# A second MLP product from seven block products instead of eight, with weights fetched in pairs

## The chip, the cores and the metric

The kernel runs on one core of a Trainium2 chip. The metric is the device time of one execution in microseconds. Before the change the median of 3 runs is 866.44 us (865.52 to 868.4).

## The reference, cut to what matters

Two layers, each a mixing sublayer and a squared-ReLU MLP, over 256 tokens of width 1024, all in float32. The change is in the second product of the MLP; the mixing sublayer (a convolution branch and two attentions, gated and projected) keeps its arithmetic.

```python
for l in range(DEPTH):                      # DEPTH = 2
    u = x @ w_in[l]
    ...                                     # y_a: convolution, y_b, y_c: attention
    m = gates[:, :, 0] * y_a + gates[:, :, 1] * y_b + gates[:, :, 2] * y_c
    x = layer_norm(DEEPNORM_ALPHA * x + m @ w_o[l], ln1_g[l], ln1_b[l])
    h = jnp.square(jax.nn.relu(x @ w_ff1[l] + b_ff1[l]))        # 256 x 4096
    x = layer_norm(DEEPNORM_ALPHA * x + h @ w_ff2[l] + b_ff2[l], ln2_g[l], ln2_b[l])
```

## The kernel before, in words

Every float32 operand of a large product is split into two float32r parts, hi and lo, whose sum is the float32 value, and each product is three matmuls (`mm3`: lo·hi, hi·lo, hi·hi). ScalarE writes hi (a cast), VectorE writes lo (a subtraction).

Weights come as units of 128 x 1024 (512 KB). `Weights.get` gives each its own raw tile (ring of RAWS = 4), hi tile and lo tile (rings of NW = 8), issues the DMA on SyncE, the cast on ScalarE and the subtraction on VectorE. In the trace these are `raw`, `whi`, `wlo`. Tiles tagged `big` (16 slots of 128 x 1024) hold the stream, its transposed split X, the hidden layer's split H, norm rows and the like; `zz` are scratch tiles; `pm`, `pa` and `pt` are the 2 + 4 + 2 PSUM banks.

A layer goes: convolution input (48 matmuls of 512 columns for each of the two token tiles), v, then q and k in `tunit`s (two chunks of 128 output columns: 48 matmuls of 256 columns from two weight units), attention beside them, gates and branch projections, output projection, first norm, MLP. In the MLP the first six 128-column chunks of the hidden layer are made with tokens on partitions and transposed; then a loop over i = 3 to 15 runs `do2(i - 3)`, 24 matmuls of 512 columns (2 k tiles, 2 token tiles, 2 halves of the output, 3 each), and a `tunit` with `hsplit(i)`, which turns two chunks into squared-ReLU and its hi and lo. The last six k tiles are done first for token tile 0, then for token tile 1 (36 matmuls each), so that the norm of tile 0 (`ln_tok`) runs while TensorE works on tile 1. The norm of a tile ends in transposes that give the next layer's X.

The order of instructions on each engine is not the order of the source. `Plan` records all instructions, computes a latest start for each from its own costs, and issues them by list scheduling: on each engine the ready instruction with the earliest latest start goes first. At run time each engine works through its list strictly in that order. Nearly every instruction is recorded through a helper, so the trace gives L122 for all; groups are told apart by their tiles.

Of the kernel before, what the change touches and what calls it, by code (L numbers as in the profile page):

```python
# [24 lines left out]
RAWS = 4  # L25
WARM = 4
NW = 8
# [13 lines left out]
class Plan:  # L41
    """Records instructions with the regions that they read and write, orders them by list
    scheduling (the one whose result is needed first goes first) and issues them in that order.
    Tile adds the waits and gives out the buffers."""
# [189 lines left out]
    def order(self):  # L234
# [20 lines left out]
        def need(op):  # L255
            """when the buffers that the instruction is first to use are free, None if unknown"""
            tm = 0.0
            new = [k for k in op.tiles if k not in where]
            seen = {}
            for k in new:  # L260
                tag = self.tiles[k]["tag"]
                j = seen.get(tag, 0)
                if self.tiles[k]["turn"] != turn[tag] + j or len(free[tag]) <= j:
                    return None
                seen[tag] = j + 1
                tm = max(tm, free[tag][j])
            return tm
# [63 lines left out]
class Weights:  # L331
    """Streams the weight units in the order of use: each lands in SBUF once and is split
    into two float32r parts whose sum is the float32 value."""
# [7 lines left out]
    def get(self, **dims):  # L341
        plan, i = self.plan, self.i
        self.i += 1
        raw = plan.tile(self.pool, [P, 1024], F32, "raw", RAWS)
        hi = plan.tile(self.pool, [P, 1024], F32R, "whi", NW)
        lo = plan.tile(self.pool, [P, 1024], F32R, "wlo", NW)
        n = 512 if i < 3 else 1024
        for c in range(0, 1024, n):
            s = slice(c, c + n)
            plan.SP.dma_start(raw[:, s], self.order[i][:, s])  # L350
            plan.Activation.copy(hi[:, s], raw[:, s])
            plan.DVE.tensor_sub(lo[:, s], raw[:, s], hi[:, s].bitcast(F32))
        pat = "p (" + " ".join(list(dims) + ["n"]) + ") -> p " + " ".join(list(dims) + ["n"])
        return [a.rearrange(pat, **dims) for a in (hi, lo)]
# [3 lines left out]
def kernel(ctx: ExitStack, tc: tile.TileContext, x, xT, w_in, w_p2, w_o, w_f1, w_f2,  # L358
# [22 lines left out]
    def split(hi, lo, src, scale=1.0):  # L381
        """hi + lo = scale * src"""
# [8 lines left out]
    def mm3(o, a, b, start, stop):  # L391
        """o += a.T @ b with a, b = (hi, lo)"""
# [62 lines left out]
    def x_at(X, kt, cols=slice(0, SEQ)):  # L455
        """(hi, lo) of k tile kt"""
# [3 lines left out]
    def rstd_of(var, n=1, eps=EPS, scale=1.0):  # L460
        """(scale * var + eps) ** -0.5"""
# [9 lines left out]
    def ln_tok(t, banks, resid, alpha, gb, dst, transposed):  # L471
        """dst = LN(alpha * resid + banks) * g + b, and its transposed split."""
        y = slot(F32, "y")
        st = R.tile(small, [P, 2, 6], F32, "st", 2)
        for h in range(2):
            s = slice(h * 512, (h + 1) * 512)
            R.DVE.scalar_tensor_tensor(y[:, s], in0=resid[:, s], scalar=alpha, in1=banks[h],
                                           op0=ALU.mult, op1=ALU.add)
# [25 lines left out]
    for l in range(L):  # L504
# [23 lines left out]
        def tunit(ticks=True):  # L528
            ps = bank()
            for c in range(2):  # L530
                w = W.get(k=KT)
                for kt in range(KT):
                    mm3(ps[:, c * 256:(c + 1) * 256], at(w, ALLP, kt), x_at(X, kt), kt == 0,
# [13 lines left out]
        # conv: gated input, then taps as background work  # L547
# [14 lines left out]
        wc = [W.get(k=2) for _ in range(8)]  # L562
# [26 lines left out]
        wv = [W.get(k=2) for _ in range(8)]  # L589
        V = [[None] * NT for _ in range(2)]  # L590
        for t in range(NT):
            for b in range(2):
# [5 lines left out]
                V[b][t] = R.tile(work, [P, 512], F32, "v", 4)  # L598
                R.Activation.copy(V[b][t], ps)

        # q, k with rotary
# [18 lines left out]
        def attn_scores(b, pair):  # L620
            """masked softmax numerators of two heads (maps), and 1 / row sums"""
# [20 lines left out]
        def transp(src):  # L642
            """[queries, keys] blocks (q1k0, q1k1, q0k0) -> (k0: q0 q1 | k1: q1), split"""
# [6 lines left out]
        # differential attention, head h  # L650
# [56 lines left out]
        # MoBA with one block: heads 2j, 2j + 1  # L707
# [39 lines left out]
        for b in range(2):  # L747
            for u in range(2):
                for w in 'qk':
                    ps = tunit()  # L750
                    d = R.tile(work, [P, 512], F32, "qk", 7)
# [48 lines left out]
        macc = [None, None]  # L800
        M = None
        for bi, gofs in ((0, 8), (1, 16), (2, 0)):
# [17 lines left out]
            for u in range(4):  # L820
                w = W.get(c=2, k=4)
                ps = bank()
                for c in range(2):
                    for kt in range(4):
                        mm3(ps[:, c * 256:(c + 1) * 256], at(w, ALLP, c, kt), at(br, ALLP, kt),
# [18 lines left out]
        gb1 = load_row(l, 0), load_row(l, 1)  # L844
        wo = [W.get(k=1) for _ in range(8)]
        X = x_new()
        for t in range(NT):
# [6 lines left out]
            ln_tok(t, ps, xtok[t], ALPHA, gb1, xtok[t], X)  # L854

# [1 line left out]
        H = {}  # L857

        def hsplit(i, ps):
            """chunks 2i, 2i + 1 of the hidden layer"""  # L860
            r = R.tile(work, [P, 1024], F32, "zz", 3)[:, :512]
            for c in range(2):
                n = 2 * i + c
                R.Activation.activation(r[:, c * 256:(c + 1) * 256], ps[:, c * 256:(c + 1) * 256],
# [157 lines left out]
```

## Time and profile before

| what | us |
|---|---|
| median of 3 runs | 866.44 |
| span of the profiled execution, first to last instruction | 867.0 |
| its time outside this span | not listed by the profile |
| TensorE (PE) busy | 852.5 |
| VectorE (DVE) busy | 624.7 |
| ScalarE (ACT) busy | 512.9 |
| GpSimd (POOL) busy | 20.6 |

The mean granted TensorE clock is 0.998 of full speed. The profiled span is 0.56 us above the median of the runs. TensorE's busy time comes from records whose ends overlap (a 512-column matmul is listed with about 0.39 us, but the next one starts 0.23 us later), so what a matmul costs is read from start to start: a stretch of the chain divided by its count. The same holds for VectorE, where a record lasts a little longer than the distance to the next start. DMA moved 157.06 MB, 181 GB/s on average.

### The profile page before, as it was taken

The page shows a single profiled execution, that of the slowest core. Times are in us where ns is not written, and L with a number is a line of the kernel's source. Part 1 is how long each engine was busy: PE and PEld are TensorE (multiplying, and loading weights), DVE is VectorE, ACT ScalarE, POOL GpSimd, SP SyncE. Part 2 cuts the span into 40 slices and gives each one's busy share as a digit, 9 for nine tenths or more (in the row PEclk, how much of TensorE's full clock was granted, in tenths as well). Part 3 has the DMA queues.
Part 4 walks back from the last instruction along what each step waited for, and adds up shares of the span by engine and source line. Part 5 has one row for each costly group of instructions (what it writes and reads, how often), then busy time and mean ns, then how long its engine had stood idle before and what let it go on. Part 6 is the DMA issues. An engine that isn't in the chain of part 4 may idle for free.

```text
span 867.0 us, 14603 instructions
## 1 busy us (share of the span) xinstructions
PE 852.5 (98%) x5704; PEld 781.1 (90%) x5704; DVE 624.7 (72%) x1011; ACT 512.9 (59%) x854; POOL 20.6 (2%) x26
## 2 busy tenths in 40 slices
PE   8999999999999999999999999999999999999996
PEld 7899989999989999999887999999998899999995
DVE  5789999985686645544588899998766874554445
ACT  5578898447347555555354788964472675555540
POOL 0000010000000000000000001000000000000000
PEclk9999999999999999999999999999999999999999
DMA  8874425554637755655365843345554686655621
GB/s 325 286 237 160 152 98 169 159 184 151 215 114 249 283 182 193 188 181 190 98 198 171 263 147 124 121 157 183 172 171 145 203 299 203 193 189 180 191 73 50
DMA packets 44422, 157.06 MB, mean 181 GB/s; under 512 B 4929, under 2 KB 5441, under 8 KB 44353
## 3 DMA queue, kind: packets, MB, share of 16 engines
q1 hardware_dynamic: 44352, 156.13, 55.4%
q8 instruction: 45, 0.74, 0.3%
q14 instruction: 25, 0.20, 0.1%
HBM read 155.06 MB, written 1.05 MB: 180 GB/s over the span
## 4 chain that ended last, share of the span: by engine, by line
PE 88%; DVE 6%; DMA 2%; ACT 2%; issue 1%; POOL 1%; DVEq 0%; ACTq 0%
PE pm L122 56%; PE pa L122 31%; DVE wlo L122 2%; DVE big L122 2%; DMA raw<-in_w_f_dram 1%; ACT zz L122 1%; DVE zz L122 1%; POOL col L122 1%; DMA raw<-in_w_in_dram 1%; DVE pt L122 1%; PE pt L122 1%; DMA big<-in_xT_dram 0%; ACT whi L122 0%; DVE qk L122 0%; DVE col L122 0%
## 5 line engine op out<-in xcount | busy, mean ns | idle before, releaser
L122 DVE TENSOR_TENSOR wlo<-raw,whi 128x1024 fp32r<-128x1024 f32 (+1 forms) x283 | 341.7, 1211 | 155.8 <-ACT whi L122 154.1
L122 PE MATMUL pm<-big,whi 128*128 128x256 f32 x2496 | 452.6, 283 | 0.0
L122 ACT CAST whi<-raw 128x1024 fp32r<-128x1024 f32 (+1 forms) x283 | 293.8, 1044 | 241.9 <-PE pm L122 169.9
L122 PEld LDWEIGHTS pm<-big,whi 128*128 128x128 f32 x2496 | 388.9, 192 | 1.3
L122 PE MATMUL pm<-big,wlo 128*128 128x256 f32 x1248 | 357.5, 286 | 0.0
L122 PEld LDWEIGHTS pm<-big,wlo 128*128 128x128 f32 x1248 | 239.0, 192 | 3.1
L122 PE MATMUL pa<-whi,big 128*128 128x512 f32 x704 | 225.1, 393 | 1.1 <-DVE big L122 1.1
L122 PEld LDWEIGHTS pa<-whi,big 128*128 128x128 f32 x704 | 133.1, 189 | 28.6 <-ACT whi L122 1.7
L122 PE MATMUL pa<-wlo,big 128*128 128x512 f32 x352 | 138.1, 392 | 0.0
L122 DVE SCALAR_TENSOR_TENSOR big<-hpad,half,big 128x256 f32<-128x256 f32 x240 | 103.5, 477 | 0.1
L122 PE MATMUL pm<-whi,big 128*128 128x512 f32 (+1 forms) x320 | 92.5, 370 | 0.0
L122 PEld LDWEIGHTS pa<-wlo,big 128*128 128x128 f32 x352 | 66.7, 190 | 12.8
L122 PEld LDWEIGHTS pm<-whi,big 128*128 128x128 f32 x320 | 58.3, 188 | 10.3 <-ACT zz L122 0.4
L122 PE MATMUL pm<-wlo,big 128*128 128x512 f32 (+1 forms) x160 | 59.3, 371 | 0.0
L122 ACT COPY zz<-pm 32x512 f32<-32x512 f32 (+1 forms) x72 | 40.8, 566 | 14.4 <-DVE zz L122 9.8
L122 DVE TENSOR_TENSOR big<-zz,big 128x512 fp32r<-128x512 f32 x32 | 22.1, 691 | 28.3 <-ACT big L122 28.3
L122 ACT ACTIVATE pt<-pt,col 128x256 f32<-128x256 f32 (+1 forms) x96 | 41.4, 461 | 0.8 <-DVE col L122 0.3
L122 POOL TENSOR_TENSOR col<-col,mhalf 128x1 f32<-128x1 f32 (+1 forms) x20 | 20.0, 1001 | 788.6 <-DVE col L122 788.6
L122 PEld LDWEIGHTS pm<-wlo,big 128*128 128x128 f32 x160 | 30.2, 189 | 4.8
L122 ACT CAST big<-pt 128x512 fp32r<-128x512 f32 x12 | 6.9, 591 | 35.8 <-PE pt L122 35.5
L122 DVE SCALAR_TENSOR_TENSOR big<-big,pa 128x512 f32<-128x512 f32 x16 | 11.0, 685 | 19.7 <-PE pa L122 19.5
L122 ACT ACTIVATE zz<-pm,cols 128x256 f32<-128x256 f32 x52 | 21.6, 465 | 4.7 <-PE pm L122 4.7
(79 smaller groups left out, 453.6 us busy)
## 6 DMA issues: line engine op xcount, KB each, us to landing
raw<-in_w_f_dram SPq DMA_DIRECT2D x128, 512.0 KB, 4.1
raw<-in_w_in_dram SPq DMA_DIRECT2D x109, 512.0 KB, 3.8
raw<-in_w_p_dram SPq DMA_DIRECT2D x24, 512.0 KB, 3.5
raw<-in_w_o_dram SPq DMA_DIRECT2D x16, 512.0 KB, 3.6
big<-in_rows_dram SPq DMA_DIRECT2D x10, 512.0 KB, 6.1
raw<-in_w_in_dram SPq DMA_DIRECT2D x6, 256.0 KB, 5.2
big<-in_xT_dram SPq DMA_DIRECT2D x4, 256.0 KB, 5.3
big<-in_x_dram SPq DMA_DIRECT2D x2, 512.0 KB, 8.1
```

The lines of the kernel that those rows point to most:

```text
L122: op.fn = lambda: fn(*args, **kw)
```

## The change: what it does

The product h @ w_ff2 is cut in two along tokens, along k within each pair of k tiles, and along output columns, and the eight block products are replaced by seven (a Strassen form with shared sums). For one pair of k tiles that is 21 matmuls of 512 columns in place of 24, and 16 pairs make a layer. For it VectorE forms four sums of weight blocks (`t`, 128 x 2048) and four differences of blocks of the hidden layer, and these are split into hi and lo like everything else: per pair of k tiles 1536 columns of plain blocks and 2048 columns of sums, where before there were two units of 1024. `hsplit` splits 896 columns where it split 512.

Weights are fetched two units into one raw tile of 128 x 2048 (RAWS = 3) and split from it, in halves of 1024 in the mixing sublayer and in one piece of 2048 in the MLP. Raw tiles apart, all weight tiles, the sums, v and the q and k tiles (until now in tiles of their own) share one ring `ws` of 11 tiles of 128 x 2048. In the list of VectorE, `ws_a<-raw_b,ws_c` is a subtraction that writes lo.

Seven accumulators take seven PSUM banks through the loop. The last DEFER = 3 pairs leave out products 7 and 4, which are recorded behind the norm of token tile 0. The norm's input is no longer one VectorE operation for each half: `fill0` and `fill1` combine the seven accumulators with the stream.

```diff
-RAWS = 4
+RAWS = 3
-NW = 8
+NW = 11
+DEFER = 3
@@ Weights
+    def split(self, raw, c0=0, c1=2048, step=2048):
+        hi, lo = self.tile(), self.tile()
+        for c in range(c0, c1, step):
+            s = slice(c, min(c + step, c1))
+            self.plan.Activation.copy(hi[:, s], raw[:, s])
+            self.plan.DVE.tensor_sub(lo[:, s], raw[:, s], hi[:, s].bitcast(F32))
+        return hi, lo
...
+    def products(self):
+        plan = self.plan
+        raw = self.load()
+        b = raw.rearrange("p (b n) -> p b n", b=4)
+        bh, bl = self.split(raw, 512)
+        t = self.tile(F32)
+        t4 = t.rearrange("p (b n) -> p b n", b=4)
+        plan.DVE.tensor_add(t4[:, 0:3:2], b[:, 1:4:2], b[:, 0:1].broadcast_to([P, 2, 512]))
+        plan.DVE.tensor_add(t4[:, 1], t4[:, 0], b[:, 3])
+        plan.DVE.tensor_add(t4[:, 3], t4[:, 1], b[:, 2])
+        th, tl = self.split(t)
...
@@ hsplit
-            t = slot(name="h").rearrange("p (s n) -> p s n", s=2)
-            H[i] = (t[:, 0], t[:, 1])
-            split(*H[i], r)
+            R.Activation.activation(f[:, 512:1024], r, AF.Square)
+            R.DVE.tensor_sub(b[:, 0:2], b[:, 5:7], b[:, 7:8].broadcast_to([P, 2, P]))
+            R.DVE.tensor_add(b[:, 2], b[:, 6], b[:, 0])
+            R.DVE.tensor_sub(b[:, 3], b[:, 2], b[:, 4])
+            hi, lo = slot(name="h"), slot(name="h")
+            split(hi[:, 0:896], lo[:, 0:896], f[:, 0:896])
@@ the loop of the MLP
-        for i in range(3, 16):
-            do2(i - 3)
-            ps = tunit()
-            hsplit(i, ps)
-        last = [W.get(k=1) for _ in range(6)]
-        for h in range(2):
-            for j in range(6):
-                ff2(26 + j, last[j], 0, h)
+        FACTORS = {1: ("a11", "b11"), 2: ("a12", "b21"), 3: ("s4", "b22"), 4: ("a22", "t4"),
+                   5: ("s1", "t1"), 6: ("s2", "t2"), 7: ("s3", "t3")}
...
+        for i in range(3, 19):
+            w = W.products()
+            for q in (1, 2, 3, 5, 6):
+                ff2(q, i - 3, w)
+            if i - 3 >= 16 - DEFER:
+                last[i - 3] = w
+            else:
+                for q in (7, 4):
+                    ff2(q, i - 3, w)
+            if i < 16:
+                hsplit(i, tunit(step=2048))
...
+        def fill0(h, y):
+            if h == 0:
+                R.Activation.copy(q1, Q[1])
+                R.DVE.tensor_add(y, r[0][0], Q[2])
+                R.DVE.tensor_add(y, y, q1)
+            else:
+                R.DVE.tensor_sub(u, Q[6], q1)
+                R.DVE.tensor_add(y, r[0][1], u)
+                R.DVE.tensor_sub(y, y, Q[5])
+                R.DVE.tensor_sub(y, y, Q[3])
...
+        ln_tok(0, fill0, gb2, xtok[0], X)
+        for q in (7, 4):
+            for i in last:
+                ff2(q, i, last[i])
+        ln_tok(1, fill1, gb2, xtok[1], X)
```

What that does to VectorE's list in the loop is seen in one round. Before, a round of the loop of layer 0 reads (`wlo`: lo of a weight unit, `big<-zz`: lo of the hidden layer):

```order
L122 TENSOR_TENSOR big_670<-zz_669,big_670 128x512
L122 TENSOR_TENSOR wlo_703<-raw_701,whi_702 128x1024
L122 TENSOR_TENSOR wlo_706<-raw_704,whi_705 128x1024
L122 TENSOR_TENSOR wlo_710<-raw_708,whi_709 128x1024
L122 TENSOR_TENSOR wlo_713<-raw_711,whi_712 128x1024
```

With the change, from one subtraction for a `tunit`'s weights to the next (`zz`: hidden-layer differences, `ws_602`: the sums, `ws_603` and `ws_604`: their hi and lo):

```order
L123 TENSOR_TENSOR zz_582<-zz_582 128x256
L123 TENSOR_TENSOR ws_601<-raw_599,ws_600 128x1536
L123 TENSOR_TENSOR ws_602<-raw_599 128x2x512
L123 TENSOR_TENSOR zz_582<-zz_582 128x128
L123 TENSOR_TENSOR ws_602<-ws_602,raw_599 128x512
L123 TENSOR_TENSOR zz_582<-zz_582 128x128
L123 TENSOR_TENSOR ws_602<-ws_602,raw_599 128x512
L123 TENSOR_TENSOR big_584<-zz_582,big_583 128x896
L123 TENSOR_TENSOR ws_604<-ws_602,ws_603 128x2048
L123 TENSOR_TENSOR ws_608<-raw_606,ws_607 128x2048
```

Four subtractions of 1024 columns and one of 512 have become ten instructions, and the subtraction `ws_604` needs a cast (`ws_603`, on ScalarE) of all four sums, the last of which is two rows above it.

At the end of the loop of layer 0, VectorE's list before reads (`pa_592`, `pa_593`: the accumulators of token tile 0; `big_811`, `big_812`: lo of the next layer's X):

```order
L122 TENSOR_TENSOR big_790<-zz_789,big_790 128x512
L122 SCALAR_TENSOR_TENSOR big_813<-big_84,pa_592 128x512
L122 BN_STATS st_814<-big_813 128x6
L122 SCALAR_TENSOR_TENSOR big_813<-big_84,pa_593 128x512
L122 BN_STATS st_814<-big_813 128x6
L122 BN_AGGR col_742_815<-st_814 128x2
L122 TENSOR_SCALAR col_743_816<-col_742_815 128x1
L122 SCALAR_TENSOR_TENSOR big_813<-big_813,col_742_815,big_590 128x512 x2
L122 SCALAR_TENSOR_TENSOR big_84<-big_813,col_744_817,big_591 128x512 x2
L122 TENSOR_TENSOR big_811<-pt_818,big_809 128x4x128
```

With the change, from the last subtraction of sums on (`pa_468` to `pa_471`: products 3, 5, 6 and 7; `ws_702` to `ws_708`: the next layer's first weights; the list goes on with three more weight subtractions, the norm's last four operations and `big_675`, `big_676`, lo of X):

```order
L123 TENSOR_TENSOR ws_672<-ws_670,ws_671 128x2048
L123 TENSOR_TENSOR ws_702<-raw_700,ws_701 128x1024
L123 TENSOR_TENSOR big_85<-big_85,pa_469 128x512
L123 TENSOR_TENSOR zz_677<-pa_470,zz_677 128x512
L123 TENSOR_TENSOR ws_702<-raw_700,ws_701 128x1024
L123 TENSOR_TENSOR big_678<-big_84,zz_677 128x512
L123 TENSOR_TENSOR zz_677<-zz_677,pa_471 128x512
L123 TENSOR_TENSOR big_678<-big_678,pa_469 128x512
L123 TENSOR_TENSOR ws_705<-raw_703,ws_704 128x1024
L123 TENSOR_TENSOR big_678<-big_678,pa_468 128x512
L123 TENSOR_TENSOR ws_705<-raw_703,ws_704 128x1024
L123 BN_STATS st_679<-big_678 128x6
```

The norm of token tile 0 used to take one operation on a finished accumulator for each half; now its second half is put together from products 5, 6 and 3 behind the last subtraction of sums, with subtractions for the next layer between the steps.

## Rows read from the trace of the kernel before

**Rows 1.** The page, part 1: span, and busy time, share and instructions of engines.
```profile
span 867.0 us, 14603 instructions
...
PE 852.5 (98%) x5704; PEld 781.1 (90%) x5704; DVE 624.7 (72%) x1011; ACT 512.9 (59%) x854; POOL 20.6 (2%) x26
```

**Rows 2.** Busy time by stretch: attention (112:158) and the loop of layer 0 (275:416.7).
```profile
core 0: us, PE busy (x) PEld busy (x) DVE busy (x) ACT busy (x) POOL busy (x), PEclk, DMA share, GB/s
112.00:158.00 46.00, 45.98 (x353) 42.55 (x352) 45.04 (x110) 38.24 (x101) 2.15 (x2) 1.00 0.46 139
275.00:416.70 141.70, 141.70 (x903) 129.28 (x902) 75.25 (x68) 78.59 (x103) 0.00 (x0) 1.00 0.63 202
```

**Rows 3.** The chain that ended last: start us, us, what, with the matmul count.
```profile
274.94 5.47 PE pa L122 x24
...
287.54 5.75 PE pm L122 x48
...
416.71 12.72 PE pa L122 x56
430.55 8.87 PE pa L122 x39
...
700.87 5.47 PE pa L122 x24
```

**Rows 4.** Groups of instructions by shape: busy us, mean ns, idle before.
```profile
L122 DVE TENSOR_TENSOR wlo<-raw,whi 128x1024 fp32r<-128x1024 f32 x277 | 337.6, 1222 | 155.4 <-ACT whi L122 153.8
L122 ACT CAST whi<-raw 128x1024 fp32r<-128x1024 f32 x277 | 290.1, 1053 | 241.2 <-PE pm L122 169.9 <-PE pa L122 38.5 <-DMA raw<-in_w_in_dram 13.0
...
L122 DVE TENSOR_TENSOR big<-zz,big 128x512 fp32r<-128x512 f32 x32 | 22.1, 691 | 28.3 <-ACT big L122 28.3
...
L122 ACT CAST big<-zz 128x512 fp32r<-128x512 f32 x32 | 20.1, 629 | 0.8
```

**Rows 5.** VectorE in order of time, first norm of layer 0: start, duration, idle.
```profile
228.87 0.68 DVE L122 SCALAR_TENSOR_TENSOR big<-big,pm 128x512 f32<-128x512 f32 x1
229.47 1.22 DVE L122 TENSOR_TENSOR wlo<-raw,whi 128x1024 fp32r<-128x1024 f32 x1
...
246.11 0.68 DVE L122 SCALAR_TENSOR_TENSOR big<-big,pa 128x512 f32<-128x512 f32 x1
...
247.43 3.48 DVE L122 TENSOR_TENSOR wlo<-raw,whi 128x1024 fp32r<-128x1024 f32 x3
251.03 0.69 DVE L122 SCALAR_TENSOR_TENSOR big<-big,pa 128x512 f32<-128x512 f32 x1
...
253.80 2.73 DVE L122 SCALAR_TENSOR_TENSOR big<-big,col,big 128x512 f32<-128x512 f32 x4
...
258.72 1.28 DVE L122 TENSOR_TENSOR big<-pt,big 128x512 fp32r<-128x512 f32 x2
```

**Rows 6.** All engines in order of time, inside the loop: a cast and its subtraction.
```profile
301.67 1.05 ACT L122 CAST whi<-raw 128x1024 fp32r<-128x1024 f32 x1 [1.83 <-PE pm L122]
...
302.75 1.23 DVE L122 TENSOR_TENSOR wlo<-raw,whi 128x1024 fp32r<-128x1024 f32 x1 [1.65 <-ACT whi L122]
```

**Rows 7.** VectorE in order of time, second norm of layer 0.
```profile
424.94 0.69 DVE L122 SCALAR_TENSOR_TENSOR big<-big,pa 128x512 f32<-128x512 f32 x1 [1.08 <-PE pa L122]
...
426.70 2.73 DVE L122 SCALAR_TENSOR_TENSOR big<-big,col,big 128x512 f32<-128x512 f32 x4
...
432.62 0.68 DVE L122 TENSOR_TENSOR big<-pt,big 128x512 fp32r<-128x512 f32 x1
```

**Rows 8.** The chain that ended last, its end, layer 1.
```profile
854.91 4.09 PE pa L122 x18
...
859.03 0.70 DVE big L122
...
862.12 0.74 DVE big L122
862.86 0.66 DVEq L1018
```

More of the change, by code (lines that the diff above doesn't have):

```diff
@@ L339, in __init__, with tile @@
         self.i = 0
[L341 to L352, printed above, removed]
-        pat = "p (" + " ".join(list(dims) + ["n"]) + ") -> p " + " ".join(list(dims) + ["n"])
-        return [a.rearrange(pat, **dims) for a in (hi, lo)]
+    def tile(self, dtype=F32R, tag="ws", bufs=NW):
+        return self.plan.tile(self.pool, [P, 2048], dtype, tag, bufs)
@@ new lines, in load @@
+    def load(self, n=1024):
+        raw = self.tile(F32, "raw", RAWS)
+        for u in range(2):
+            for c in range(0, 1024, n):
+                self.plan.SP.dma_start(raw[:, u * 1024 + c:u * 1024 + c + n],
+                                       self.order[self.i][:, c:c + n])
+            self.i += 1
+        return raw
+    def split(self, raw, c0=0, c1=2048, step=2048):
[5 more added lines that the diff above has]
+        return hi, lo
@@ new lines, in get2, with take @@
+    def get2(self, step=1024, **dims):
+        first = self.i < 4
+        raw = self.load(512 if first else 1024)
+        pair = self.split(raw, step=512 if first else step)
+        pat = "p (" + " ".join(list(dims) + ["n"]) + ") -> p " + " ".join(list(dims) + ["n"])
+        return [[a[:, u * 1024:(u + 1) * 1024].rearrange(pat, **dims) for a in pair]
+                for u in range(2)]
+    def take(self, n, step=1024, **dims):
+        return [w for _ in range(n // 2) for w in self.get2(step, **dims)]
@@ L560, in tap @@
                                                op0=ALU.mult, op1=ALU.add)
-        wc = [W.get(k=2) for _ in range(8)]
+        wc = W.take(8, k=2)
         pp = [[bank("pa"), bank("pm")] for _ in range(NT)]
@@ L586 @@
                 R.bias = 0.0
-        wv = [W.get(k=2) for _ in range(8)]
+        wv = W.take(8, k=2)
+        vt = W.tile(F32)
         V = [[None] * NT for _ in range(2)]
@@ L597 @@
                         kt == 0, kt == KT - 1)
-                V[b][t] = R.tile(work, [P, 512], F32, "v", 4)
+                V[b][t] = vt[:, (2 * b + t) * 512:(2 * b + t + 1) * 512]
                 R.Activation.copy(V[b][t], ps)
@@ L747 @@
         for b in range(2):
+            qk = W.tile(F32)
             for u in range(2):
-                for w in 'qk':
+                for i, w in enumerate('qk'):
                     ps = tunit()
-                    d = R.tile(work, [P, 512], F32, "qk", 7)
+                    d = qk[:, (2 * u + i) * 512:(2 * u + i + 1) * 512]
                     rope(ps, d)
@@ L844 @@
         gb1 = load_row(l, 0), load_row(l, 1)
-        wo = [W.get(k=1) for _ in range(8)]
+        wo = W.take(8, k=1)
         X = x_new()
@@ L909, in tick, with ff2 @@
+        Q = {}
+        for q in (1, 2, 3, 5, 6, 7, 4):
+            Q[q] = bank("pt" if q < 3 else "pm" if q == 4 else "pa")
+        def ff2(q, i, w):
+            a, b = FACTORS[q]
+            mm3(Q[q], H[i][a], w[b], i == 0, i == 15)
         def tick():
             pass
-        for i in range(3, 16):
-            do2(i - 3)
-            ps = tunit()
-            hsplit(i, ps)
-        last = [W.get(k=1) for _ in range(6)]
-        for h in range(2):
-            for j in range(6):
-                ff2(26 + j, last[j], 0, h)
@@ L920 @@
[L920 to L925 removed]
+        last = {}
+        for i in range(3, 19):
[9 more added lines that the diff above has]
+                hsplit(i, tunit(step=2048))
@@ new lines @@
+        X = x_new() if l < L - 1 else None
+        qq = R.tile(work, [P, 1024], F32, "zz", 3)
+        q1, u = qq[:, :512], qq[:, 512:]
+        r = [[xtok[t][:, h * 512:(h + 1) * 512] for h in range(2)] for t in range(NT)]
+        def fill0(h, y):
[8 more added lines that the diff above has]
+                R.DVE.tensor_sub(y, y, Q[3])
@@ L927, with fill1 @@
+        def fill1(h, y):
+            if h == 0:
+                R.DVE.tensor_sub(r[1][1], r[1][1], Q[5])
+                R.DVE.tensor_sub(u, u, Q[7])
+                R.DVE.tensor_sub(y, r[1][0], u)
+                R.DVE.tensor_add(y, y, Q[4])
+            else:
+                R.DVE.tensor_add(y, r[1][1], u)
+        ln_tok(0, fill0, gb2, xtok[0], X)
[3 more added lines that the diff above has]
+        ln_tok(1, fill1, gb2, xtok[1], X)
     for t in range(NT):
```

62 lines of the change are left out of this document (32 added, 30 removed).

## The prediction, made before the run

> **What bounds the kernel now.** I read the busy shares first, then the stretches, the chain, the groups by shape and last the single instructions. TensorE is busy for 852.5 of 867.0 us [rows 1], and in the loop of layer 0 for all 141.7 us at a granted clock of 1.00, while VectorE is busy for 75.25 [rows 2]. The chain alternates between 24 matmuls of 512 columns in 5.47 us, 0.228 us each, and 48 of 256 columns in 5.75 us, 0.120 us each [rows 3]. A round is therefore 11.22 us, all TensorE, and VectorE has about half of it free. The large idle time in front of VectorE's subtractions is put down to ScalarE's casts (153.8 us) [rows 4]; in the loop it costs nothing now. The question is whether it still costs nothing once VectorE's half-empty rounds are filled.
>
> **Matmuls removed.** 3 of 24 in each of 16 pairs and 2 layers: 96 x 0.228 = 21.9 us of TensorE's path. With nothing else in the way a round is 21 x 0.228 + 5.75 = 10.54 us. The second product of layer 0 ends now at 416.71 + 72 x 0.228 + 0.9 for eight transposes in between = 434.0; the next layer's convolution starts right there (430.55 + 8.87 - 24 x 0.228 = 433.9) [rows 3]. With 48 matmuls fewer TensorE alone would be through at 423.0.
>
> **VectorE's work added.** What an operation costs in a full queue is the distance of starts, not its duration. One of 512 columns takes 0.60 (228.87 to 229.47); of 1024 columns, three in a row take 3.48 and the last of them 1.22, so 1.13 each [rows 5]. That is 0.53 for 512 more columns, and I go along this line to the sizes that the trace does not show: 2048 columns 2.19, 1536 1.66, 896 1.00, 256 0.33, 128 0.20. For 2048 the bounds are 4 x 0.53 = 2.12 (columns alone) and 2 x 1.22 = 2.44 (two of the shown ones, full duration [rows 4]); I take 2.19, on the line of the starts. A broadcast operand is not shown either: between 1.13 and two of 0.69 for the sum of 1024 columns; I take 1.13, the nearest shape.
> A round is now: plain blocks 1.66, sums 1.13 + 0.60 + 0.60, their subtraction 2.19, the `tunit`'s weights 2.19, hidden layer 0.33 + 0.20 + 0.20 + 1.00. Together 10.1 us, against 4 x 1.13 + 0.60 = 5.1 before. This alone fits under TensorE's 10.54, with 0.44 us to spare.
>
> **The wait added.** The subtraction of the sums waits for one cast of all four sums, and that cast for the last sum. A cast of 1024 columns takes 1.05, of 512 0.63 [rows 4], so 2048 take 1.05 + 2 x 0.42 = 1.90. A subtraction starts 0.03 after its cast ends (301.67 + 1.05, then 302.75) [rows 6]; for the step from VectorE to ScalarE I take 0.05. From the start of the last sum: 0.69 + 0.05 + 1.90 + 0.03 = 2.67, of which the sum itself takes 0.60 of the queue. In the remaining 2.07 VectorE can only do what its list has between the two. In the 15 pairs behind the first that is a piece of 128 columns six times (1.87 idle), the 896-column subtraction five times (1.07 idle), and in the other four 0.93, 0.94, nothing and 1.37. Sum 19.8 us in a layer. Queued behind the waiting instruction are the next `tunit`'s weights, which TensorE waits for. A round is then 10.1 + 1.55 = 11.65 us: longer than TensorE's 10.54, and longer than the 11.22 of before. Below, the wait could cost nothing, if VectorE were so far ahead that TensorE never saw it; but VectorE is the slower one in each round, so a lead is used up, by 1.1 us a round.
>
> **The start of the loop.** In the first norm VectorE's list has 3.48 + 1.13 us of weight subtractions between 246.11 and the norm's last operations, which end at 253.80 + 2.73 = 256.5 [rows 5]. Now there are 2048 + 2048 + 1536 + 1024 + 512 columns, 7.8 us, so these end some 3.3 us later, at 259.8. Then the last sum (0.69), two casts of the transposed X (1.08 together, as two of 0.63 that overlap a little [rows 4]), the cast of the sums (1.90), their subtraction (2.19) and the second half of X's lo (0.60), where before X's lo was written from 258.72 on [rows 5]: 266.3. From there to the last subtraction of sums the list has 13 x 2.19 for `tunit`s, 15 x 6.18 for pairs, 16 x 1.73 for the hidden layer, two stream operations of 1.13 and three of 0.60: 153.0 us. With 19.8 of waiting VectorE is through at 439.1, 16 us behind the 423.0 that TensorE could do. The last three pairs have no `tunit`: 8 to 10 us of VectorE each against 4.8 of TensorE.
>
> **The norm behind the loop.** Now tile 0's norm starts at 424.94 and its X is written at 432.62 [rows 7], under the 36 matmuls of tile 1 (8.2 us), so it costs nothing. After the change products 5, 6 and 3 end only with the last pair, so the norm starts behind 439.1, and the 18 deferred matmuls (4.1 us) are mostly in front of it in TensorE's list. VectorE's list then holds eight weight subtractions of 1.13, six combining operations and one of statistics at 0.60, 0.2 of small ones, the norm's 2.73 (as at 426.70 [rows 7]) and some 0.5 of dependent starts: 16.7 us to X. The convolution of layer 1 starts at 455.8 instead of 433.9: 21.9 us lost in layer 0. Its 48 matmuls (10.9 us) then cover tile 1's norm (10.7 by the same count).
> In layer 1 everything is 21.9 us late and, by the distance of the two loops (700.87 - 274.94 = 425.93 [rows 3]), the last subtraction falls at 439.1 + 425.9 + 21.9 = 886.9. No weights follow there: nine combining operations, three of statistics, eight of the norms at about 0.66, 0.4 of small ones and 0.9 of waiting give 13.8. Behind the last one stand the same 3.5 us as now (862.86 + 0.66 to 867.0 [rows 1, 8]). Span 904.2; the median of the runs shown lies 0.6 below its span, so 904.
>
> **Costed at nothing.** ScalarE's larger casts: about 7.5 us a round, beside VectorE's 10.1. DMAs: as many, of the same size, two to a raw tile, and GpSimd's power for the norms is unchanged. The shared ring in the mixing sublayer: 11 tiles less v and two of q and k are 4 pairs, the 8 units of before. There VectorE is busy for 45.04 of 46 us [rows 2]; TensorE idles 0.02 there, so nothing is to be gained, and if one pair came late the loss would be one `tunit`, 5.75 us a layer. I take none.
> The clock: every stretch shown has 1.00 [rows 2], but none has TensorE waiting for 14 us, as now between the layers. If it fell to half there, the 48 matmuls of the convolution would take up to 10.9 us more. None is taken; it is in the range.
> The Trainium skill, VectorE: DVE Perf Modes, section on the DRAIN you can't avoid, says that the next operation does not start until the pipe has emptied (and that one which is not held starts earlier); taken strictly, each would hold the queue for its whole duration. Here three subtractions of 1222 ns took 3.48 us, not 3.67 [rows 4, 5], and the sum goes by that. By the rule the time would be that of the third rival.
>
> **The rivals.** (1) The waits for the sums' casts don't show, because other work fills them. VectorE is then through at 419.3, TensorE at 423.0, and only the norm behind the loop is left: X at 439.7, 5.8 late, and layer 1 ends at 423.0 + 425.9 + 5.8 + 13.8 + 3.5 = 872. For it speaks that 153.0 us of work is no more than TensorE's own; against it that each engine keeps its list's order. (2) Faster: TensorE stays the bound, which holds as long as a wait is under 0.44 us a round, and the norm is put together as accumulators finish, beside the 18 deferred matmuls. Then 21.9 go, and come back only the norm's 8.4 us (424.94 to 433.3 [rows 7]) with three more operations (1.8) less 4.1 of cover in layer 0, and some 2 us at the end: 867.0 - 21.9 + 6.1 + 2 = 853. For it speaks VectorE's idle half in the loop; against it the five splits for the next layer between the steps of that norm, and 1.55 us of wait a round. (3) VectorE's operations don't overlap: 0.09 more for each of some 145 in a layer's loop, 26 us in both: 930. (4) Gain and losses cancel: 867.
>
> **How the numbers follow.** My forecast 0.60, with its own range 886 to 920; rival 1 0.13; rival 2 0.14; rival 3 0.08; rival 4 0.05. About 0.3%, 2.6 us, is what a measurement here can tell from no change. Faster has rival 2, 0.14; the same has rival 4, 0.05; slower has the rest, 0.81. The range from 866 to 930 leaves out rival 2 and the outer halves of 3 and 4, 0.2 in all.
>
> **What would show it.** In the loop after the change: rounds of about 11.6 us instead of 11.2, VectorE busy for nearly all but 1 to 2 us in each, idle in front of the 2048-column subtraction of sums and waiting there for ScalarE; TensorE with gaps of about 1 us a round in front of the sums' matmuls, larger in the last three pairs. Between the layers a gap of some 14 us in which TensorE does only transposes. I am wrong if TensorE's rounds are 10.5 us without gaps, or if the convolution of layer 1 starts within a few us of the last product.

## The result, and the profile after

The changed kernel takes 962.06 us (median of 4 runs, 961.35 to 963.06) against 866.3 us: a ratio of 1.1103, 95% interval 1.1089 to 1.1116. The prediction was 904, with 930 as its upper end: the sign was right, the loss more than twice as large. The profiled execution has a span of 961.3 us.

The page of the kernel after, part 1, answers to [rows 1]:

```profile
span 961.3 us, 14325 instructions
...
PE 865.1 (90%) x5608; PEld 777.7 (81%) x5608; DVE 785.2 (82%) x1186; ACT 549.5 (57%) x825; POOL 20.3 (2%) x26
```

The 96 matmuls are gone (5704 to 5608), and yet TensorE is busy for 12.6 us longer: for part of the time it runs at the lower of its two clock levels (1.2 instead of 2.4 GHz). The idle share went from 2% to 10%. Where, is seen by marking the same places in both traces: the first matmul of the output projection, of the MLP's loop (`pt<-ws,big`) and of the next layer's convolution (starts, in us, as the chain that ended last has them).

| stretch | before | after | more |
|---|---|---|---|
| start to output projection, layer 0 (mixing) | 228.3 | 240.9 | 12.6 |
| to the first product of the loop | 46.6 | 51.7 | 5.1 |
| loop and norm, to the convolution of layer 1 | 159.0 | 190.4 | 31.4 |
| to output projection, layer 1 (mixing) | 221.0 | 235.8 | 14.8 |
| to the first product of the loop | 45.9 | 51.7 | 5.8 |
| loop and norm, to the end | 166.1 | 190.7 | 24.6 |

The six add up to the 94.3 us between the spans. The mixing sublayer, whose ring the prediction had costed at nothing, lost 27.4.

**The mixing sublayer.** Busy time by stretch, kernel after (columns as in [rows 2]); the first two lie in v, q and k of layer 0, the last between the layers, and the two lines behind them are the same places of q and k before:

```profile
33.00:63.00 30.00, 24.74 (x132) 21.28 (x130) 27.18 (x60) 10.52 (x15) 0.00 (x0) 1.00 0.37 132
63.00:114.00 51.00, 45.03 (x331) 43.30 (x333) 43.35 (x94) 34.55 (x69) 1.61 (x1) 0.87 0.39 145
466.00:483.00 17.00, 5.23 (x16) 3.74 (x15) 16.55 (x23) 9.23 (x12) 0.91 (x1) 0.60 0.53 185
```
```profile
33.00:63.00 30.00, 30.00 (x175) 26.59 (x173) 26.42 (x40) 18.93 (x23) 0.00 (x0) 1.00 0.72 230
63.00:114.00 51.00, 49.45 (x410) 47.58 (x409) 46.54 (x119) 43.61 (x99) 3.22 (x2) 1.00 0.48 157
```

TensorE now idles here, and from 63 to 114 us, behind the first gap, its granted clock is 0.87 on average, which mixes stretches at 2.4 and at 1.2 GHz; before it was 1.00. TensorE in order of time (start, duration, operation, idle before and who ended it):

```profile
51.83 5.91 PE L123 MATMUL pm<-big,ws 128*128 128x256 f32 x48
63.78 17.18 PE L123 MATMUL pm<-big,ws 128*128 128x256 f32 x120 [6.04 <-DVE ws L123]
...
99.77 13.48 PE L123 MATMUL pm<-big,ws 128*128 128x256 f32 x96 [3.11 <-DVE ws L123]
```

The first `tunit` of q ends at 57.74, and the weights of the next are not there. ScalarE and VectorE tell why:

```profile
52.03 0.59 ACT L123 COPY ws<-pm 128x512 f32<-128x512 f32 x1 [4.85 <-PE pm L123]
57.78 0.58 ACT L123 COPY zz<-pm 32x512 f32<-32x512 f32 x1 [5.16 <-PE pm L123]
59.12 1.75 ACT L123 COPY zz<-pm 32x512 f32<-32x512 f32 x3 [0.76 <-DVE zz L123]
60.89 5.78 ACT L123 CAST ws<-raw 128x1024 fp32r<-128x1024 f32 x6
```
```profile
39.93 16.72 DVE L123 SCALAR_TENSOR_TENSOR big<-hpad,half,big 128x256 f32<-128x256 f32 x42
...
61.91 0.68 DVE L123 TENSOR_TENSOR ws<-zz 128x512 f32<-128x512 f32 x1
62.51 6.89 DVE L123 TENSOR_TENSOR ws<-raw,ws 128x1024 fp32r<-128x1024 f32 x6
```

VectorE does 42 convolution taps in a row meanwhile. The six casts at 60.89 come behind the rotary copies (`zz<-pm`), although their weights had landed long before: no DMA is issued between 41 and 64.9 us. The tile that takes the rotated q and k (`ws<-zz`) is one of the shared ring, and `Plan` hands out a ring strictly in the order in which its tiles are first recorded (`need`: a tile whose turn is not next returns None). The first rotary write stands in the recording between the first and the second `tunit`'s weights. So these weights can only have a tile after an operation that waits for TensorE's first `tunit`. Layer 1 has the same gaps of 6.04 and 3.11 us.

**The loop.** The later rounds are nearly as predicted, 11.87 us each over seven of them (359.38 to 442.44) against 11.65. The five before them average 14.0 (289.21 to 359.38): VectorE also writes lo of the first three hidden pairs there and waits for them. Groups by shape, kernel after, answering to [rows 4]:

```profile
L123 DVE TENSOR_TENSOR ws<-ws,ws 128x2048 fp32r<-128x2048 f32 x32 | 73.3, 2292 | 40.1 <-ACT ws L123 39.4 <-PE pa L123 0.7
...
L123 DVE TENSOR_TENSOR ws<-raw,ws 128x1536 fp32r<-128x1536 f32 x32 | 56.0, 1751 | 1.6 <-issue 1.6
...
L123 ACT CAST ws<-ws 128x2048 fp32r<-128x2048 f32 x32 | 60.9, 1903 | 56.9 <-DVE ws L123 56.9
```

One round of VectorE, with the wait for the sums' cast at both ends (1.77 idle, then 1.76, 12.0 us apart):

```profile
359.38 2.29 DVE L123 TENSOR_TENSOR ws<-ws,ws 128x2048 fp32r<-128x2048 f32 x1 [1.77 <-ACT ws L123]
361.59 1.08 DVE L123 TENSOR_TENSOR big<-zz,big 128x896 fp32r<-128x896 f32 x1
362.59 3.95 DVE L123 TENSOR_TENSOR ws<-raw,ws 128x2048 fp32r<-128x2048 f32 x2
366.46 1.22 DVE L123 TENSOR_TENSOR ws<-raw 128x1024 f32<-128x1024 f32 x1
...
371.39 2.29 DVE L123 TENSOR_TENSOR ws<-ws,ws 128x2048 fp32r<-128x2048 f32 x1 [1.76 <-ACT ws L123]
```

The two ends of the loop, TensorE in order of time:

```profile
283.78 0.44 PE L123 MATMUL pa<-cst,zz 128*128 128x128 f32 x2 [0.52 <-ACT zz L123]
292.65 2.90 PE L123 MATMUL pt<-ws,big 128*128 128x512 f32 x6 [8.43 <-DVE big L123]
...
465.66 2.93 PE L123 MATMUL pa<-ws,big 128*128 128x512 f32 x6 [1.13 <-DVE ws L123]
468.38 0.88 PE L123 MATMUL pm<-ws,big 128*128 128x512 f32 x2
479.49 1.97 PE L123 MATMUL pt<-cst,big 128*128 128x128 f32 x8 [10.23 <-DVE big L123]
483.03 7.11 PE L123 MATMUL pa<-ws,big 128*128 128x512 f32 x24 [1.56 <-DVE big L123]
```

The 10.23 and 1.56 between the layers are the gap foreseen, 14 us with the transposes. The 8.43 in front of the first product is not in the prediction: it waits for lo of the first hidden pair, which VectorE writes behind the subtraction of the second pair's sums.

### The profile page after: what moved, and what is told of

Its sections match the earlier page's. It is cut to its first block, busy times and chain, and to the rows that moved or that the text cites. A ratio compares the mean times of both kernels' runs of the same rounds, so it can differ in the third digit from the quotient of the medians.

```text
span 961.3 us, 14325 instructions
## 1 busy us (share of the span) xinstructions
PE 865.1 (90%) x5608; PEld 777.7 (81%) x5608; DVE 785.2 (82%) x1186; ACT 549.5 (57%) x825; POOL 20.3 (2%) x26
## 4 chain that ended last, share of the span: by engine, by line
PE 66%; DVE 17%; ACT 10%; issue 5%; DMA 1%; DVEq 0%; ACTq 0%
PE pm L123 49%; PE pa L123 15%; DVE ws L123 11%; ACT ws L123 6%; ACT zz L123 3%; DVE big L123 3%; PE pt L123 3%; DVE zz L123 2%; DMA big<-in_xT_dram 1%; ACT pt L123 1%; ACT big L123 1%; DVE pt L123 0%; DVE st L123 0%; DVE am L123 0%; DVE col L123 0%
## 5 line engine op out<-in xcount | busy, mean ns | idle before, releaser
L123 PE MATMUL pm<-big,ws 128*128 128x256 f32 x3744 | 473.4, 287 | 19.1 <-DVE ws L123 19.1
L123 PEld LDWEIGHTS pm<-big,ws 128*128 128x128 f32 x3744 | 463.4, 195 | 26.0 <-DVE ws L123 13.5
L123 DVE TENSOR_TENSOR ws<-raw,ws 128x1024 fp32r<-128x1024 f32 (+2 forms) x220 | 310.4, 1432 | 51.9 <-issue 32.9
L123 ACT CAST ws<-raw 128x1024 fp32r<-128x1024 f32 (+2 forms) x220 | 262.7, 1221 | 90.9 <-PE pm L123 58.1
L123 PE MATMUL pa<-ws,big 128*128 128x512 f32 x672 | 181.8, 415 | 25.9 <-ACT ws L123 13.3
L123 PEld LDWEIGHTS pa<-ws,big 128*128 128x128 f32 x672 | 131.0, 199 | 65.5 <-DVE ws L123 18.7
L123 PE MATMUL pm<-ws,big 128*128 128x512 f32 (+1 forms) x576 | 134.9, 376 | 1.5 <-DVE big L123 1.5
L123 PEld LDWEIGHTS pm<-ws,big 128*128 128x128 f32 x576 | 103.4, 191 | 21.8 <-DVE big L123 2.0
L123 DVE TENSOR_TENSOR ws<-ws,ws 128x2048 fp32r<-128x2048 f32 x32 | 73.3, 2292 | 40.1 <-ACT ws L123 39.4
L123 ACT CAST ws<-ws 128x2048 fp32r<-128x2048 f32 x32 | 60.9, 1903 | 56.9 <-DVE ws L123 56.9
L123 PEld LDWEIGHTS pt<-ws,big 128*128 128x128 f32 x192 | 35.9, 200 | 28.0 <-issue 17.3
```

The source lines that it names most:

```text
L123: op.fn = lambda: fn(*args, **kw)
```

## The experiments

All ratios are to the kernel before (866 to 867 us), run beside it.

**mix_only and late_turn: was the mixing sublayer's loss the ring, and what in it?** mix_only puts the second MLP product back and keeps pairs and ring. late_turn takes the changed kernel and lets q and k's tile have its turn behind the next weights:

```diff
+        nxt = W.get2(k=KT)
         for b in range(2):
             qk = W.tile(F32)
             for u in range(2):
                 for i, w in enumerate('qk'):
-                    ps = tunit()
+                    ps = tunit(ww=nxt)
+                    if (b, u, w) != (1, 1, 'k'):
+                        nxt = W.get2(k=KT)
```

> The changed kernel with the second MLP product as it was before (eight block products, 4 banks, one weight unit per k tile): only the fetching and splitting by pairs, the shared ring of 11 tiles and 3 raw pairs are left of the change. Theory A (the sublayer of conv, attention and gates lost its time to the ring, not to the MLP): that sublayer keeps its +12.6 us in layer 0 and +14.8 us in layer 1, its MLP takes what it took before (205.7 and 212.1 us), so 866.3 + 27.4 = 894 us, between 885 and 900. Rival B (what was lost there is a consequence of the MLP's new order, through the planner's due times): about 866 us. Rival C (pairs cost the old MLP loop too, because a unit waits for its partner's landing): over 900 us.

> The changed kernel, with one edit: in the q and k part the weights of the next unit pair are recorded before the rotary step of the present one, so that the shared tile for q and k takes its turn in the ring behind the next pair's weights and not ahead of them. Theory A (the qk tile's turn: the first rotary write of a qk tile can only follow TensorE's first product of q, and all later weights' casts stand behind it in the ring): the gap of TensorE of 6.0 us at 57.8 to 63.8 us goes, a good part of the gaps of 5.1 us between 93 and 100 us and the granted clock of 0.87 from 63 to 114 us (6.6 us of 51) go with them; with the same in layer 1 some 15 to 25 us less than 962, so 937 to 947 us. Rival B (pairs: a unit of TensorE's work waits for two casts and two subtractions instead of one): the gaps stay, 958 to 966 us.

mix_only: 895.5 us, ratio 1.0334 (1.0312 to 1.0356); 29 us lost with the old MLP, the same 6.03 us gap in its trace. late_turn: 930.64 us (1.0716 to 1.0755), 31.4 less than the change, more than I gave it. In the traces 28.4 us of it lie in the two mixing sublayers, the rest in the loops. The same stretches of late_turn:

```profile
33.00:63.00 30.00, 30.00 (x175) 26.58 (x175) 26.52 (x57) 12.44 (x19) 0.00 (x0) 1.00 0.48 171
63.00:114.00 51.00, 50.63 (x422) 48.92 (x420) 47.22 (x112) 45.41 (x103) 1.77 (x2) 1.00 0.48 169
```

TensorE is busy for 80.63 of these 81 us, and the clock stays at 1.00. The ring's size and the pairs stayed as they were; only the order of recording, and with it the turn, was changed. Theory A holds for the cause; it gave the edit too small a gain.

**mix_late: does anything of pairs and ring cost time besides?** mix_only with the edit of late_turn.

> The kernel of mix_only (pairs and shared ring, the second MLP product as before) with the edit of late_turn. Theory A (all that pairs and the shared ring cost is the turn of the q and k tile): 895.5 - 31.4 = 864 us, so within 862 to 868 us, no different from before or a little faster. Rival B (the shared ring costs the old MLP loop or the gates something too): 870 us or more.

865.64 us against 866.88, ratio 0.9989 (0.998 to 0.9997). Nothing else does that this run could tell from no change. It is the only version that is not slower than before, and its gain of 1.2 us is less than the 0.3% I had called no change.

**sums_1024: is the wait for the one cast worth what VectorE's idle time says?**

```diff
-        th, tl = self.split(t)
+        th, tl = self.split(t, step=1024)
```

> The changed kernel, the tile of the sums t1 to t4 cast and subtracted in two pieces of 1024 columns instead of one of 2048. Theory A (VectorE's rounds of 11.6 us hold a wait of 1.4 us on average for ScalarE's one cast of 1.90 us; TensorE's round is 10.54 us): the wait falls to about half, at 0.15 us of added subtraction, rounds near TensorE's 10.6 us, so 7 to 10 us less in each layer: 942 to 950 us. Rival B (VectorE's own work of 10.1 us and the chains behind it bound the round, and a shorter wait is taken up elsewhere): 957 to 964 us.

925.37 us (1.0659 to 1.07): 36.7 less than the change. Both theories gave it too small a gain; A's sign is right, its size is half. The groups of sums_1024:

```profile
L123 DVE TENSOR_TENSOR ws<-ws,ws 128x1024 fp32r<-128x1024 f32 x64 | 76.4, 1220 | 4.8 <-ACT ws L123 3.3
L123 DVE TENSOR_TENSOR ws<-raw,ws 128x2048 fp32r<-128x2048 f32 x32 | 73.3, 2289 | 17.9 <-ACT ws L123 10.8 <-PE pa L123 6.9
```

Idle in front of the sums' subtractions fell from 40.1 to 4.8 us, not by half: while the second piece is cast, VectorE subtracts the first. But 12 us of idle moved to the `tunit`'s subtraction (5.6 us in the kernel after): there VectorE now waits in part for TensorE, which has become the longer one. So these 35 us are not the gain itself. What VectorE gained is seen from its first subtraction of 2048 columns to its last subtraction of sums, in each layer; first the kernel after, then sums_1024:

```profile
241.55:465.61 224.06, 185.72 (x194) 0.96 0.48 165
719.50:943.52 224.02, 185.72 (x193) 0.96 0.43 151
```
```profile
241.12:452.12 211.00, 188.88 (x213) 0.98 0.50 175
698.44:906.57 208.13, 185.96 (x209) 0.98 0.45 162
```

That is 29.0 of the 38.1 us between the two spans (961.3 and 923.2). Another 7.5 lie behind the last subtraction of sums of layer 0: from there to the convolution it is 9.95 us (452.12 to 462.07) instead of 17.4. The new pieces changed the order of VectorE's list too, and three subtractions of the next layer's weights are left there where the kernel after has eight. So part of what this edit won is the norm's, not the wait's.

**no_sums: what remains if the sums cost nothing?** The three adds and the split of `t` are left out; plain blocks stand in place of the sums, so TensorE's work is the same and the result is another.

```diff
-        bh, bl = self.split(raw, 512)
-        t = self.tile(F32)
...
-        th, tl = self.split(t)
+        bh, bl = th, tl = self.split(raw)
```

> The changed kernel without the sums of weight blocks: the three adds and the second split are left out, and the products that should take t1 to t4 take blocks of the raw pair's split in their place, so the numbers differ; TensorE's work and the fetches are the changed kernel's. VectorE's round falls from 10.1 to 5.8 us, ScalarE's by 1.5 us. Theory A (the sums and their split are what the seven products cost in the loop, and TensorE would give back 11 us a layer): the MLP falls to some 11 us a layer below the kernel before, while conv, attention and gates keep their +27.4 us: 866.3 + 27.4 - 21.9 = 872 us, up to 885 us with the chain of the first three hidden pairs in front of the loop. Rival B (a good part is lost to the start of the loop, the norm behind it and the clock that falls there, whatever the weights cost): 905 to 930 us.

906.82 us (1.0443 to 1.0484): rival B. In place of TensorE's 8.43 and 10.23 its trace has gaps of 5.53 and 7.54, which are therefore not made by the sums of weights.

**both and unit_first: are these losses separate, and is the start of the loop one more?** both has the edits of late_turn and sums_1024. unit_first adds to it that in a round the hidden unit pair goes ahead of the products (`hsplit(i, tunit(step=2048))` at the head of the loop body, the units fetched in that order).

> The edits of late_turn and of sums_1024 together. Theory A (they are two losses in two places, the q and k part and the MLP's loop): their gains add, 31.4 + 36.7 us off 962.1, so 894 us, between 890 and 899. Rival B (both runs won the same thing, the granted clock of TensorE after a gap): well under the sum, over 905 us.

> The kernel of 'both', and in the MLP's loop the hidden unit pair of a round comes ahead of the products of the round, not behind them, so that 48 matmuls of 256 columns (5.7 us) lie between the first three hidden pairs and the first products. Theory A (TensorE's gap at the loop's start, 8.4 us in the changed kernel and 6.1 us with the sums in two pieces, is the chain of relu, square, four VectorE sums, cast and subtraction of the first hidden pair, and these matmuls hide it): 5 to 6 us less a layer, so 880 to 886 us. Rival B (the gap is the first sums' split on VectorE, which is only put off): 891 to 897 us.

both: 896.62 us (1.0326 to 1.0361). The gains add to within 3 us. unit_first: 887.3 us (1.022 to 1.025), 9.3 less; it missed its range by 1.3. TensorE at the start of unit_first's loop:

```profile
269.38 4.43 PE L123 MATMUL pm<-big,ws 128*128 128x256 f32 x35
275.93 1.63 PE L123 MATMUL pt<-ws,big 128*128 128x512 f32 x6 [2.12 <-DVE big L123]
```

The gap is 2.12 instead of 6.1 us, after 48 matmuls more: the chain of the first hidden pair is somewhat longer than what was put beside it.

**unit_first_2048: the same start, with VectorE as the longer engine.** late_turn with the edit of unit_first, the sums in one piece.

> The kernel of late_turn with the hidden unit pair of a round ahead of the round's products, the sums still cast in one piece of 2048 columns. It asks what the start of the loop is worth when VectorE, not TensorE, is the longer one behind it. Theory A (VectorE bounds the loop: its own idle time at the start counts, 5.6 us a layer behind ScalarE's relu, square and cast of the first hidden pairs and 1.1 us behind a bank): up to 6 us less a layer, 918 to 927 us. Rival B (TensorE's gap of 8.4 us at the start is lost time by itself): 17 us less than 930.6, 911 to 917 us. Rival C (the loop has VectorE's full work whatever comes first): 928 us or more.

917.08 us (1.0556 to 1.0594), 13.6 less than late_turn, between the ranges of A and B. The 5.6 + 1.1 us of VectorE's waits that A starts from make 13.4 in two layers; I had rounded them down. A whole gap of TensorE's (B) is more than was gained. VectorE's waits from its first subtraction of 2048 columns to the last subtraction of sums, layer 0, show which went; first late_turn, then unit_first_2048:

```profile
DVE big L123 <- ACT big L123: 5.1, 6, 1.8
DVE zz L123 <- ACT zz L123: 2.4, 4, 1.3
```
```profile
DVE big L123 <- ACT big L123: 1.1, 1, 1.1
```

The waits for ScalarE's relu, square and cast of hidden pairs fell by 6.4 us, those for TensorE by no more than about 1 us, and 2 us more are spent on casts of weights. By these rows the clock behind TensorE's gap has little part in the gain.

**all_no_sums: what would seven products give with everything else mended?** no_sums with the edits of late_turn and unit_first.

> The kernel of no_sums (the weight sums and their split left out, other blocks in their place, so the numbers differ) with the edits of late_turn and unit_first: what the seven products could give if their sums cost nothing. Theory A (losses add): 906.8 - 31.4 - 2 x 5.5 = 864 us, between 860 and 869, about the kernel before: of the 21.9 us that TensorE saves, most goes to the norm behind the loop. Rival B (only the sums stand between the change and its 21.9 us): 845 to 855 us.

871.32 us (1.0035 to 1.0065), 2.3 us above theory A's range and far from B. TensorE at the end of its layer 0:

```profile
423.25 2.20 PE L123 MATMUL pm<-ws,big 128*128 128x512 f32 x9
432.76 1.94 PE L123 MATMUL pt<-cst,big 128*128 128x128 f32 x8 [7.31 <-DVE big L123]
436.20 4.02 PE L123 MATMUL pa<-ws,big 128*128 128x512 f32 x10 [1.50 <-DVE big L123]
```

From the last product (425.45) to the convolution pass 10.75 us in which TensorE only transposes; before, it had matmuls of token tile 1 there [rows 3, 7]. That is as much as the 11 us which 48 matmuls fewer had saved in this layer. So even with sums that cost nothing this form comes out no faster than before.

**norm_first and best512: can the norm be moved, are smaller pieces better?** norm_first is unit_first with the norm's operations ahead in the lists (`R.bias = -20000` around both `ln_tok`); best512 casts the sums in pieces of 512 besides.

> The kernel of unit_first, with the operations of the norm behind the MLP's loop put ahead of the other work in VectorE's and ScalarE's lists (in the list of the order two of the five subtractions for the next layer's weights move behind steps of the norm). Theory A (the norm of the first 128 tokens, whose VectorE operations stand between such subtractions, holds up TensorE at the end of layer 0, where it has two gaps of 2.3 and 5.3 us at a granted clock of 0.6 to 0.7): 2 to 5 us less than 887.3, so 882 to 885 us. Rival B (the chain of the norm itself is the length): 886 to 889 us.

> The kernel of norm_first with the sums cast and subtracted in four pieces of 512 columns instead of two of 1024. Theory A (in unit_first VectorE's wait for the sums' casts is down to 2.2 us a layer, and the pieces add 0.14 us of VectorE a round): no gain, within 3 us of norm_first, 882 to 889 us. Rival B (TensorE waits for the last piece of a pair near the loop's end, where it has no lead, and smaller pieces come earlier): 875 to 881 us.

norm_first: 891.58 us (1.0273 to 1.0304), 4 us worse than unit_first, outside both ranges. best512: 887.0 us (1.0221 to 1.0249), inside A's range, but 4.6 better than norm_first where A allowed 3, and no better than unit_first. The trace of norm_first shows 2.7 of its 4 us between the layers, where the convolution starts at 445.12 instead of 442.44. VectorE's last subtraction of sums ends earlier, at 430.18 instead of 432.49, but six subtractions of the next layer's weights stand behind it and ahead of X, where unit_first has three: the edit put more of them into the way of the norm, not fewer. No version with seven products that also forms the sums had a median below 887.

**pool_sums: the three adds on GpSimd.** The kernel of both, with `plan.Pool.tensor_tensor(..., op=ALU.add)` for the sums.

> The kernel of 'both' with the three adds of the weight sums (2.58 us of VectorE's work a round) on GpSimd. Theory A (with the sums cast in two pieces TensorE bounds the rounds, and only their start and the last three pairs still wait for VectorE): 3 to 8 us less than 'both' (894 expected there), so 886 to 891 us. Rival B (GpSimd's adds take longer than they save, being on the chain from a landing to the sums' cast, and the two engines slow each other down): over 900 us. The trace of before has no GpSimd operation of this size, so the rows decide.

964.17 us (1.1103 to 1.116): rival B. GpSimd and VectorE in two stretches of its loop:

```profile
325.67 2.38 POOL L123 TENSOR_TENSOR ws<-raw 128x1024 f32<-128x1024 f32 x1 [5.44 <-DVE ws L123]
325.94 7.03 DVE L123 TENSOR_TENSOR ws<-raw,ws 128x2048 fp32r<-128x2048 f32 x2 [0.35 <-ACT ws L123]
328.13 5.99 POOL L123 TENSOR_TENSOR ws<-ws,raw 128x512 f32<-128x512 f32 x2
```
```profile
349.12 2.39 POOL L123 TENSOR_TENSOR ws<-raw 128x1024 f32<-128x1024 f32 x1 [1.13 <-DMA raw<-in_w_f_dram]
...
350.00 2.47 DVE L123 TENSOR_TENSOR big<-zz,big 128x896 fp32r<-128x896 f32 x1 [1.07 <-ACT big L123]
```

The two subtractions that took 3.95 in the kernel after take 7.03 here. Over the whole run a subtraction of 2048 columns (`ws<-raw,ws`) takes 3.15 us on average, where it took 2.29.

## Why the prediction was wrong in size, point by point

- **"The shared ring in the mixing sublayer ... I take none": the step that failed most.** I counted how many tiles are free and not in which order they are given out. late_turn shows 31.4 us for the turn alone; the sublayer's gaps, 6.04 and 3.11 us in each layer, and the clock of 0.87 behind them are the parts that the trace shows. The bound of "one `tunit`, 5.75 us a layer" had the right mechanism (one pair late) and the wrong count: it happens at each of the two q and k tiles, and it takes the clock with it. The sentence that TensorE idles 0.02 there, "so nothing is to be gained", argued about a gain where a loss was in question.
- **The start of the loop.** VectorE's first subtraction of a `tunit` was forecast at 266.3 and comes at 278.96, that is 266.4 if the 12.6 us of the mixing sublayer are taken off. But the waits of VectorE in the first two rounds, for relu, square and cast of three hidden pairs, are in no term: unit_first_2048 shows 13.6 us for this place in the two layers. This is the second step that failed.
- **VectorE's work: right in its prices, 4 us a layer too low in all.** 2048 columns were put at 2.19 and take 2.21 from start to start (359.38 to 361.59), 896 at 1.00 and take 1.00 (361.59 to 362.59). 153.0 us of work had been summed; from 264.81 to 449.16 in late_turn, the loop without the mixing sublayer's loss, VectorE is busy for 156.9, and in layer 1 for 157.1.
- **The wait for the cast: right.** 1.90 forecast for the cast, 1903 ns measured; 19.8 us of waiting a layer forecast, and in late_turn's loop it is 18.4:

```profile
L123 DVE TENSOR_TENSOR ws<-ws,ws 128x2048 fp32r<-128x2048 f32 x15 | 34.4, 2291 | 18.4 <-ACT ws L123 18.4
L123 DVE TENSOR_TENSOR ws<-raw,ws 128x2048 fp32r<-128x2048 f32 x13 | 29.7, 2287 | 2.7 <-ACT ws L123 1.5 <-PE pa L123 1.1
...
L123 DVE TENSOR_TENSOR big<-zz,big 128x896 fp32r<-128x896 f32 x16 | 17.4, 1086 | 3.2 <-ACT big L123 3.2
...
L123 DVE TENSOR_TENSOR zz<-zz 128x256 f32<-128x256 f32 x16 | 6.7, 420 | 2.4 <-ACT zz L123 2.4
```

  The prediction put 32 us on these waits (904 against 872 of rival 1), and sums_1024 took 36.7 off, of which 29 lie in VectorE's part and 7.5 in the norm behind it. VectorE idles for 27.4 us in this stretch; the 9.0 beside the 18.4, most of them for the hidden pairs, are the term that was left out above.
- **The norm behind the loop: right.** 16.7 us from the last subtraction of sums to X were forecast. In the kernel after it ends at 463.31 + 2.29 = 465.6, and the convolution starts at 483.03: 17.4. At the end of layer 1 17.3 were forecast (13.8 + 3.5), and it is 17.8. That this norm eats what TensorE saves in layer 0 is shown by all_no_sums.
- **The clock: named, and taken at nothing.** It is 0.60 between the layers and 0.87 in q and k. In q and k its share is inside what late_turn gave back and is not measured by itself. Between the layers it cost little: in late_turn, which still has this gap, the mixing sublayer of layer 1 takes 221.4 us (466.58 to 687.97), where it took 221.0 before. In layer 0, without such a gap ahead of it, it is 1.5 us shorter than before (226.6 against 228.1), so some 2 us, an estimate from these rows, is the most that it cost.
- **The sum.** 904 + 31.4 (turn) + 13.6 (start of the loop) = 949; 13 us of the 962 are not attributed by a run of their own. The trace of late_turn shows where they lie. Its span is 929.0 against the 904.2 that was forecast, 24.8 more. VectorE from the first subtraction of a `tunit`'s weights in the loop to the last subtraction of sums, in each layer:

```profile
264.81:449.16 184.35, 156.95 (x158) 0.97 0.47 169
726.18:911.27 185.09, 157.05 (x157) 0.96 0.42 151
```

  For this stretch 172.8 us had been summed (153.0 of work and 19.8 of waiting), so it is 23.8 us too long in the two layers: 8.0 of work and 15.8 of waiting. The waits for the sums' cast came out some 1 us a layer shorter than forecast; 9 us a layer stand in front of other instructions, 5.6 of them for the hidden pairs. The norm and the end add 0.7 and 0.5. So nearly all of the excess that is not the turn's lies in VectorE's stretch through the loop.
- **The rivals.** Rival 2 (TensorE stays the bound, 853) fails even where the sums are free: all_no_sums takes 871.3. Rival 3 (operations of VectorE don't overlap): the starts lie 2.21 apart at a duration of 2.29, so they do overlap. The time of 930 that it gave is no evidence for it: that late_turn landed on 930.6 is chance.

## What to carry to other kernels

When tiles of different lifetime are put into one ring that is handed out in order, ask of each tile which instruction takes it first and what that one waits for: all tiles behind it wait for the same. Work that is moved to an engine with room must be read with its chain: here a sum, a cast and a subtraction of one large tile put 18.4 us a layer of waiting between the engines, and halving the pieces removed nearly all of the waiting at this place, though a third of it (12 of 35 us in both layers) came up again in front of another instruction. An engine's saving at the end of a stage counts only if something is left to do there while the next stage's input is made.

## What the runs showed of the hardware that was not expected

GpSimd took 2.38 us for a sum of 1024 columns (2.94 on average over the 32 of the run) for which VectorE takes 1.22, and VectorE's subtractions took longer meanwhile. In the second stretch of pool_sums VectorE's 896 columns, 1.09 us elsewhere, took 2.47: GpSimd's sum ended at 349.12 + 2.39 = 351.51, and the subtraction 0.96 later, at 352.47, as if it had begun only then. The Trainium skill, SBUF — State Buffer, section "Who interferes with whom", says that a VectorE instruction with two SBUF inputs contends with a GpSimd instruction that reads SBUF, and that the ports which the two share are an exclusive lock on which the order of issue decides who blocks. This pair of rows agrees.

The granted clock fell behind gaps that are short against the run: 6.0 us of idle at 57.8, and from 63 to 114 us the mean is 0.87, so the first 120 matmuls of 256 columns behind it take 17.18 us, 0.143 each, where [rows 3] have 0.120.
